# Summing clipped rows: the last four rows in four loads, each shared by ScalarE and VectorE

## The chip, the cores and the metric

The kernel runs on one core of one Trainium2 chip. Its time is device time in microseconds (us), the median of several runs. A core has engines with instruction queues of their own: here ScalarE (ACT in the profile), VectorE (DVE) and SyncE (SP), which issues every DMA. TensorE and GpSimd do none of the work. Engines and DMAs are kept in order by semaphores alone: a load adds 16 to its semaphore when all its data has landed, an instruction of an engine adds 1 when its result is written.

## The reference

```python
def setup_inputs():
    batch, seq, dim = 32, 512, 1024
    return {"x": np.random.randn(batch, seq, dim).astype(np.float32)}

def reference(x):
    relu_x = np.maximum(x, 0)
    return np.sum(relu_x, axis=-1).astype(np.float32)
```

So 16,384 rows of 1,024 float32 numbers are clipped at zero and summed, row by row. 67.1 MB are read, 64 KB are written.

## The kernel before

Each of the 128 partitions holds 128 rows (NT), and its sums are gathered in `res`, a column for each row. Three buffers (`bufs`, called `io` in the profile) hold 16 rows of each partition. Seven full loads of 16 rows go round these buffers, and a load into a buffer waits for the sums of what was in it. The last 16 rows come in pieces: loads of 8 and of 4 rows (`TAIL`), and then the last four rows, which the change is about.

There are three ways to sum a row, each a small helper in `relu_sum`:

- `clamp` and `total` (lines 115 to 131): ScalarE clips many rows in place, and VectorE then adds them up, one instruction each. This is done for the first 92 rows of a partition.
- `act_row` (lines 133 to 139): ScalarE clips one row and adds it up in one instruction, ACTIVATE, with a short second one, ACTIVATION_READ_ACCUMULATOR, which writes the sum and raises the semaphore `act`.
- `dve_row` (lines 141 to 155): VectorE does the same with TENSOR_SCALAR_CACHE_REDUCE and DVE_READ_ACCUMULATOR, and raises `dve`.

The order within each queue is the order in which the program is written; there is no planner. All loads are issued by SP in order (line 99), each with a semaphore of its own, and share the 16 DMA engines of one queue, so they land in the order of issue. Behind the loads SP has three stores (`store`, lines 106 to 113). Each store is a wait for `act` as an instruction of its own (line 109) and then the DMA, which itself waits for `dve` (line 110). The first store has the sums of rows 0 to 15, the second those up to the first two of the last four rows, the third those of the last two.

The last four rows, called r0 to r3 here, are 4 x 1,024 columns in a partition. Before the change they come in four loads (lines 204 to 217), in this order:

1. 2,328 columns: r0, r1 and the first 280 of r2 (`START_PIECE`). ScalarE sums r0; VectorE sums r1 and then the 280.
2. 1,284 columns: the last 260 of r2 (`END_PIECE`) and all of r3. ScalarE sums r3, VectorE the 260.
3. 240 columns of r2, into a buffer of their own (`piece`). VectorE sums them.
4. 244 columns of r2, into another buffer. VectorE sums them (lines 226 to 235) together with three columns behind them, in which the three partial sums of r2 stand.

Clipping leaves a partial sum as it is, since it is not negative, so the last instruction gives the sum of r2. It waits for the last load in an instruction of its own and for VectorE's own partial sums in itself. ScalarE has no part in it.

Of the kernel before, what the change touches and what calls it, by code (L numbers as in the profile page):

```python
# [4 lines left out]
F32 = mybir.dt.float32  # L5
RELU = mybir.ActivationFunctionType.Relu
MAX, ADD = mybir.AluOpType.max, mybir.AluOpType.add
P = 128

ROWS = 16  # L10
# [3 lines left out]
TWO = [[16], [16], [16], [8, 8], [8, 8], [7, 7], []]  # L14
# [3 lines left out]


TAIL = [8, 4]  # L20
START_PIECE, END_PIECE = 280, 260
PIECES = [240, 244]

EARLY = 1

# [1 line left out]
def kernel(tc: tile.TileContext, x: bass.AP, out: bass.AP):  # L27
    nc = tc.nc
    sems = Semaphores(tc)

    tc.close()
    tc.compile()
    nc.cur_bb = nc.bb_map[tc.start_bb_name]
    body = nc.cur_bb.bb.instructions
    ends = list(body)
    body.clear()
    n_stores = relu_sum(nc, sems, x, out)
    body.extend(ends)


    nc.cur_bb = nc.bb_map[tc.start_bb_name + "_end"]
    nc.cur_bb.bb.instructions.clear()
    nums = sorted(s.num for s in (*sems.loads, sems.act, sems.dve))
    cleared = range(nums[0], nums[-1] + 1)
    assert len(cleared) == len(nums)
    nc.sync.sem_clear(cleared)
    nc.sync.wait_ge(sems.stored, 16 * n_stores).then_inc(sems.stored, -16 * n_stores)
    open_without_barrier(tc, EARLY)


class Semaphores:
    def __init__(self, tc: tile.TileContext):
        n = len(TWO) + len(TAIL) + 2 + len(PIECES)
        self.loads = [tc.alloc_semaphore(f"load{i}") for i in range(n)]
        self.act = tc.alloc_semaphore("act")
        self.dve = tc.alloc_semaphore("dve")
        self.stored = tc.alloc_semaphore("stored")


def relu_sum(nc, sems: Semaphores, x: bass.AP, out: bass.AP):  # L60
    x_flat = x.flatten_outer_dims()
    N, D = x_flat.shape
    NT = N // P
    NB = len(TWO)
    assert N == P * NT == P * ROWS * (NB + 1)
    assert sum(TAIL) == ROWS - 4 and START_PIECE + END_PIECE + sum(PIECES) == D

    bufs = [nc.alloc_sbuf_tensor(f"io{i}", [P, ROWS, D], F32) for i in range(NBUF)]
    res = nc.alloc_sbuf_tensor("res", [P, NT], F32)

    extra = len(PIECES) + 1
    parts = [
        nc.alloc_sbuf_tensor(f"piece{i}", [P, w + extra * (i + 1 == len(PIECES))], F32)
        for i, w in enumerate(PIECES)
    ]


    N1 = P * ROWS
# [6 lines left out]
    def rows(m, n):  # L85
        if m < ROWS:
            return xf[:, m : m + n, :]
        return xv[:, m - ROWS : m - ROWS + n, :]
# [8 lines left out]
    def load(dst, src, after=None):  # L97
        nonlocal n_load
        dma = nc.sync.dma_start(out=dst, in_=src)  # L99
        if after:  # L100
            dma.wait_op(sems.dve, after[1], "sem-ge")
        dma.then_inc(sems.loads[n_load], 16)
        n_load += 1
        return sems.loads[n_load - 1]

    def store(m, n, act, dve):
        nonlocal n_store
        dst, src = sums(m, n)
        nc.sync.wait_ge(sems.act, act)
        nc.sync.dma_start(out=dst, in_=src).wait_op(sems.dve, dve, "sem-ge").then_inc(  # L110
            sems.stored, 16
        )
        n_store += 1
# [19 lines left out]
    def act_row(ap, accum_out, loaded):  # L133
        nonlocal n_act
        i = nc.scalar.activation(out=ap, in_=ap, func=RELU, accum_out=accum_out)  # L135
        if loaded is not None:
            i.wait_op(loaded, 16, "sem-ge")
        i.then_inc(sems.act, 1)
        n_act += 1

    def dve_row(ap, accum_out, loaded):
        nonlocal n_dve
        i = nc.vector.tensor_scalar(  # L143
            out=ap,
            in0=ap,
            scalar1=0.0,
            scalar2=None,
            op0=MAX,
            op1=ADD,
            accum_out=accum_out,  # L150
        )
        if loaded is not None:
            i.wait_op(loaded, 16, "sem-ge")
        i.then_inc(sems.dve, 1)
        n_dve += 1

    freed = []
    m = 0
    for j in range(NB):
        buf = bufs[j % NBUF]  # L160
        loaded = load(buf[:, :, :], rows(m, ROWS), j >= NBUF and freed[j - NBUF])
        c = 0
# [19 lines left out]
    buf = bufs[NB % NBUF]  # L182
    c = 0
    for n in TAIL:
        loaded = load(
            buf[:, c : c + n, :], rows(m, n), None if c else freed[NB - NBUF]
        )
# [8 lines left out]
    flat = buf[:, :, :].rearrange("p c d -> p (c d)")  # L196
    src = rows(m, 4).rearrange("p c d -> p (c d)")
    at = c * D
    split = 2 * D
    b = split + START_PIECE  # L200
    end = split + D - END_PIECE
    last, w = parts[-1], PIECES[-1]
    others = [last[:, w + i : w + i + 1] for i in range(extra)]
    loaded = load(flat[:, at : at + b], src[:, :b])
    act_row(buf[:, c, :], res[:, m : m + 1], loaded)
    sums_act = n_act
    dve_row(buf[:, c + 1, :], res[:, m + 1 : m + 2], loaded)
    sums_dve = n_dve
    dve_row(flat[:, at + split : at + b], others[0], None)
    loaded = load(flat[:, at + end : at + 4 * D], src[:, end:])  # L210
    act_row(buf[:, c + 3, :], res[:, m + 3 : m + 4], loaded)
    dve_row(flat[:, at + end : at + 3 * D], others[1], loaded)
    arrived = []
    for part, n in zip(parts, PIECES):
        arrived.append(load(part[:, :n], src[:, b : b + n]))
        b += n
    assert b == end

    store(0, ROWS, *freed[0])
    store(ROWS, NT - ROWS - 2, sums_act, sums_dve)

    for i in range(len(PIECES) - 1):
        dve_row(parts[i][:, :], others[2 + i], arrived[i])
    nc.vector.wait_ge(arrived[-1], 16)
    nc.vector.tensor_scalar(  # L227
        out=last[:, :],
        in0=last[:, :],
        scalar1=0.0,  # L230
        scalar2=None,
        op0=MAX,
        op1=ADD,
        accum_out=res[:, NT - 2 : NT - 1],
    ).wait_op(sems.dve, n_dve, "sem-ge").then_inc(sems.dve, 1)
    n_dve += 1
    store(NT - 2, 2, n_act, n_dve)
    return n_store

# [48 lines left out]
```

## Time and profile before

| | |
|---|---|
| Runs | 161.22, 161.13 and 160.91 us, median 161.13 |
| Span of the profiled execution | 159.84 us |
| Its own time | not listed apart; median less span leaves 1.29 us around the span |
| DMA queue | 67.18 MB, busy 97.9% of the span |
| VectorE, ScalarE | busy 117.6 us (74%) and 104.2 us (65%) |
| Loads 1 to 4 of the last four rows, landed | 155.50, 157.15, 157.45, 157.77 us |
| Last store issued, last store landed | 158.41, 159.80 us |

The span runs from the first instruction, which is the issue of the first load, to the last. A time in the table counts from its start. A load's landing is its issue time and the time to landing that the profile lists for it; the time that an engine starts after a wait on it agrees within 0.03 us.

How to read the rows: a line of the timeline has the start, the length, the engine (ACT, DVE; SPq is SP's queue), the line of the kernel, the operation, what it writes and reads, and, in brackets, how long the engine had been idle and for what. An operation of 128x280 works on 280 columns of 128 partitions. A READ_ACCUMULATOR overlaps the end of the instruction before it, and the next instruction of the engine can begin while it runs.

### The profile page before, as it was taken

What the parts mean: (1) busy time and instruction counts of PE and PEld (TensorE: products, weight loads), DVE (VectorE), ACT (ScalarE), POOL (GpSimd) and SP (SyncE); (2) the same over time, 40 slices, a digit from 0 to 9 for tenths busy, and PEclk for the clock granted to TensorE, in tenths of its full rate; (3) what the DMA queues carried; (4) which work ended last, traced back from release to release, by engine and by line L of the source; (5) the groups of instructions that cost most, each with busy time, mean ns of one, the idle gap of its engine ahead of it and who ended that gap; (6) DMA issues with size and microseconds to landing.
All of it is one profiled execution on the core that took longest, in us unless ns stands there. A gap on an engine that the chain in (4) does not pass through costs nothing.

```text
span 159.8 us, 120 instructions
## 1 busy us (share of the span) xinstructions
DVE 117.6 (74%) x43; ACT 104.2 (65%) x50; POOL 0.2 (0%) x4
## 2 busy tenths in 40 slices
DVE  0000000006999799994999999999999999999986
ACT  0000049993699808996099951999329993499994
POOL 0000000000000000000000000000000000000000
DMA  8996996996996997999989969969969969898993
GB/s 279 508 508 279 525 508 279 525 492 295 525 492 295 525 459 328 525 394 394 525 361 426 525 295 492 525 262 525 508 279 525 508 279 525 377 410 385 425 416 102
DMA packets 2304, 67.18 MB, mean 420 GB/s; under 512 B 640, under 2 KB 896, under 8 KB 1024
## 3 DMA queue, kind: packets, MB, share of 16 engines
q1 hardware_dynamic: 2304, 67.18, 97.9%
HBM read 67.11 MB, written 0.07 MB: 420 GB/s over the span
## 4 chain that ended last, share of the span: by engine, by line
DMA 44%; DVE 33%; ACT 17%; another core or an unknown queue 3%; SPq 1%; issue 0%
DMA io<-in_x_dram 44%; DVE res L128 32%; ACT io L120 17%; SPq L99 1%; DVE io L143 0%; DVE piece L227 0%; DVE piece L143 0%
## 5 line engine op out<-in xcount | busy, mean ns | idle before, releaser
L128 DVE TENSOR_REDUCE res<-io 128x8 f32<-128x8192 f32 (+2 forms) x9 | 101.1, 11286 | 40.2 <-ACT io L120 40.2
L120 ACT ACTIVATE io<-io 128x8192 f32<-128x8192 f32 (+2 forms) x9 | 81.7, 9111 | 26.0 <-DMA io<-in_x_dram 25.9
L135 ACT ACTIVATE io<-io 128x1024 f32<-128x1024 f32 x20 | 20.9, 1044 | 6.1 <-DMA io<-in_x_dram 6.1
L143 DVE TENSOR_SCALAR_CACHE_REDUCE io<-io 128x1024 f32<-128x1024 f32 (+2 forms) x15 | 15.8, 1110 | 0.6 <-DMA io<-in_x_dram 0.4
L118 ACT ACT_TABLE_LOAD x1 | 1.3, 1283 | 22.0 <-DMA io<-in_x_dram 22.0
L135 ACT ACTIVATION_READ_ACCUMULATOR io<-io 128x1 f32 x20 | 3.7, 187 | 0.0
L143 DVE DVE_READ_ACCUMULATOR io<-io 128x1 f32 x15 | 1.2, 82 | 0.0
L227 DVE TENSOR_SCALAR_CACHE_REDUCE piece<-piece 128x247 f32<-128x247 f32 x1 | 0.4, 410 | 0.0
L143 DVE TENSOR_SCALAR_CACHE_REDUCE piece<-piece 128x240 f32<-128x240 f32 x1 | 0.4, 398 | 0.0
L272 POOL MEMSET const-bfloat16-1.0<- 128x1 bf16 x1 | 0.1, 102 | 0.0
L272 POOL MEMSET const-uint8-127<- 128x1 uint8 x1 | 0.1, 102 | 0.0
L272 POOL MEMSET const-float32-1.0<- 128x1 f32 x1 | 0.1, 99 | 0.0
L272 POOL MEMSET const-float32-0.0<- 128x1 f32 x1 | 0.1, 98 | 0.2 <-issue 0.2
L143 DVE DVE_READ_ACCUMULATOR piece<-piece 128x1 f32 x1 | 0.1, 84 | 0.0
L227 DVE DVE_READ_ACCUMULATOR piece<-piece 128x1 f32 x1 | 0.1, 83 | 0.0
## 6 DMA issues: line engine op xcount, KB each, us to landing
io<-in_x_dram SPq DMA_DIRECT2D x1, 4096.0 KB, 21.6
io<-in_x_dram SPq DMA_DIRECT2D x1, 2048.0 KB, 26.1
io<-in_x_dram SPq DMA_DIRECT2D x1, 1164.0 KB, 28.4
io<-in_x_dram SPq DMA_DIRECT2D x1, 642.0 KB, 29.6
piece<-in_x_dram SPq DMA_DIRECT2D x1, 122.0 KB, 29.2
piece<-in_x_dram SPq DMA_DIRECT2D x1, 120.0 KB, 29.4
io<-in_x_dram SPq DMA_DIRECT2D x7, 26.9
out_dram<-res SPq DMA_DIRECT2D x1, 55.0 KB, 1.6
```

The source lines that it names most:

```text
L99: dma = nc.sync.dma_start(out=dst, in_=src)
L118: nc.scalar.preload_act_table(RELU).wait_op(loaded, 16, "sem-ge")
L120: i = nc.scalar.activation(out=ap, in_=ap, func=RELU)
L128: nc.vector.tensor_reduce(out=res[:, m : m + n], in_=ap, axis=mybir.AxisListType.X, op=ADD).wait_op(sems.act, n_act, "sem-ge").then_inc(se ...
L135: i = nc.scalar.activation(out=ap, in_=ap, func=RELU, accum_out=accum_out)
L143: i = nc.vector.tensor_scalar(out=ap, in0=ap, scalar1=0.0, scalar2=None, op0=MAX, op1=ADD, accum_out=accum_out,)
L227: nc.vector.tensor_scalar(out=last[:, :], in0=last[:, :], scalar1=0.0, scalar2=None, op0=MAX, op1=ADD, accum_out=res[:, NT - 2 : NT - 1],) ...
L272: nc = _bacc.Bacc("TRN2", target_bir_lowering=False, num_devices=1)
```

## The change

The four rows still come in four loads, of other sizes and in part in another order, and both engines work on each:

1. 2,304 columns: r0 for ScalarE; r1 and the first 256 of r2 (`HEAD`) for VectorE.
2. 906 columns, the end of r3: the first 276 (`END_DVE`) for VectorE, 630 for ScalarE.
3. 531 columns of r2: 295 (`MIDDLE_DVE`) for VectorE, 236 (`MIDDLE_ACT`) for ScalarE.
4. 355 columns across the border of the two rows, into one buffer `last`: the last 237 of r2 (`LAST_DVE`) for VectorE, the first 118 of r3 (`LAST_ACT`) for ScalarE.

The buffer `last` has three columns ahead of the 355, for r2's partial sums, and two behind them, for r3's. VectorE's last instruction adds up 240 columns (3 + 237), ScalarE's 120 (118 + 2). One of r2's partial sums is now ScalarE's, and one of r3's is VectorE's. So ahead of its last instruction each of the two queues gets two waits as instructions of their own: for all of ScalarE's earlier sums, and for VectorE's (in ScalarE's queue only up to the 276 columns). The wait for the last load stands in the last instruction itself. SP's order is the same: loads, first store, second store, last store.

```diff
-START_PIECE, END_PIECE = 280, 260
-PIECES = [240, 244]
+HEAD = 256
+MIDDLE_DVE, MIDDLE_ACT = 295, 236
+LAST_DVE, LAST_ACT = 237, 118
+END_DVE = 276
...
+    n_last = LAST_DVE + LAST_ACT
+    last = nc.alloc_sbuf_tensor("last", [P, 3 + n_last + 2], F32)
...
-    loaded = load(flat[:, at : at + b], src[:, :b])
+    head = 2 * D + HEAD
+    middle = head + MIDDLE_DVE + MIDDLE_ACT
+    end = middle + n_last
+    dve_sums = [last[:, i : i + 1] for i in range(3)]
+    act_sums = [last[:, 3 + n_last + i : 4 + n_last + i] for i in range(2)]
+    loaded = load(flat[:, at : at + head], src[:, :head])
     act_row(buf[:, c, :], res[:, m : m + 1], loaded)
     sums_act = n_act
     dve_row(buf[:, c + 1, :], res[:, m + 1 : m + 2], loaded)
     sums_dve = n_dve
-    dve_row(flat[:, at + split : at + b], others[0], None)
+    dve_row(flat[:, at + 2 * D : at + head], dve_sums[0], None)
     loaded = load(flat[:, at + end : at + 4 * D], src[:, end:])
-    act_row(buf[:, c + 3, :], res[:, m + 3 : m + 4], loaded)
-    dve_row(flat[:, at + end : at + 3 * D], others[1], loaded)
-    arrived = []
-    for part, n in zip(parts, PIECES):
-        arrived.append(load(part[:, :n], src[:, b : b + n]))
-        b += n
+    split = at + end + END_DVE
+    dve_row(flat[:, at + end : split], act_sums[0], loaded)
+    ends_dve = n_dve
+    act_row(flat[:, split : at + 4 * D], act_sums[1], loaded)
+    loaded = load(flat[:, at + head : at + middle], src[:, head:middle])
+    split = at + head + MIDDLE_DVE
+    dve_row(flat[:, at + head : split], dve_sums[1], loaded)
+    act_row(flat[:, split : at + middle], dve_sums[2], loaded)
+    loaded = load(last[:, 3 : 3 + n_last], src[:, middle:end])
...
-    for i in range(len(PIECES) - 1):
-        dve_row(parts[i][:, :], others[2 + i], arrived[i])
-    nc.vector.wait_ge(arrived[-1], 16)
-    nc.vector.tensor_scalar(
-        out=last[:, :],
...
-    ).wait_op(sems.dve, n_dve, "sem-ge").then_inc(sems.dve, 1)
-    n_dve += 1
+    nc.vector.wait_ge(sems.act, n_act)
+    nc.vector.wait_ge(sems.dve, n_dve)
+    nc.scalar.wait_ge(sems.act, n_act)
+    nc.scalar.wait_ge(sems.dve, ends_dve)
+    dve_row(last[:, : 3 + LAST_DVE], res[:, NT - 2 : NT - 1], loaded)
+    act_row(last[:, 3 + LAST_DVE :], res[:, NT - 1 : NT], loaded)
     store(NT - 2, 2, n_act, n_dve)
```

More of the change, by code (lines that the diff above doesn't have):

```diff
@@ L52, in __init__ @@
     def __init__(self, tc: tile.TileContext):
-        n = len(TWO) + len(TAIL) + 2 + len(PIECES)
+        n = len(TWO) + len(TAIL) + 4
         self.loads = [tc.alloc_semaphore(f"load{i}") for i in range(n)]
@@ L65, in relu_sum @@
     assert N == P * NT == P * ROWS * (NB + 1)
-    assert sum(TAIL) == ROWS - 4 and START_PIECE + END_PIECE + sum(PIECES) == D
+    assert sum(TAIL) == ROWS - 4
+    assert HEAD + MIDDLE_DVE + MIDDLE_ACT + LAST_DVE == D
     bufs = [nc.alloc_sbuf_tensor(f"io{i}", [P, ROWS, D], F32) for i in range(NBUF)]
     res = nc.alloc_sbuf_tensor("res", [P, NT], F32)
[L71 to L75, printed above, removed]
+    n_last = LAST_DVE + LAST_ACT
+    last = nc.alloc_sbuf_tensor("last", [P, 3 + n_last + 2], F32)
     N1 = P * ROWS
@@ L198, in relu_sum @@
     at = c * D
[L199 to L203, printed above, removed]
-    loaded = load(flat[:, at : at + b], src[:, :b])
+    head = 2 * D + HEAD
[4 more added lines that the diff above has]
+    loaded = load(flat[:, at : at + head], src[:, :head])
     act_row(buf[:, c, :], res[:, m : m + 1], loaded)
@@ L208, in relu_sum @@
     sums_dve = n_dve
-    dve_row(flat[:, at + split : at + b], others[0], None)
+    dve_row(flat[:, at + 2 * D : at + head], dve_sums[0], None)
     loaded = load(flat[:, at + end : at + 4 * D], src[:, end:])
-    act_row(buf[:, c + 3, :], res[:, m + 3 : m + 4], loaded)
-    dve_row(flat[:, at + end : at + 3 * D], others[1], loaded)
-    arrived = []
-    for part, n in zip(parts, PIECES):
-        arrived.append(load(part[:, :n], src[:, b : b + n]))
-        b += n
-    assert b == end
+    split = at + end + END_DVE
[7 more added lines that the diff above has]
+    loaded = load(last[:, 3 : 3 + n_last], src[:, middle:end])
     store(0, ROWS, *freed[0])
     store(ROWS, NT - ROWS - 2, sums_act, sums_dve)
-    for i in range(len(PIECES) - 1):
-        dve_row(parts[i][:, :], others[2 + i], arrived[i])
-    nc.vector.wait_ge(arrived[-1], 16)
-    nc.vector.tensor_scalar(
-        out=last[:, :],
[L229 to L234, printed above, removed]
-    ).wait_op(sems.dve, n_dve, "sem-ge").then_inc(sems.dve, 1)
-    n_dve += 1
+    nc.vector.wait_ge(sems.act, n_act)
[4 more added lines that the diff above has]
+    act_row(last[:, 3 + LAST_DVE :], res[:, NT - 1 : NT], loaded)
     store(NT - 2, 2, n_act, n_dve)
```

## The prediction, made before the changed kernel had run

> **What bounds the kernel now.** I read the page first (span, the DMA row, the queue's share), then the chain that ended last, then the timeline of the last 5 us, the groups with their shapes kept apart for the price of an instruction by its columns, and the answers for `piece` and for the single queue waits. The page:
>
> ```profile
> span 159.8 us, 120 instructions
> DMA  8996996996996997999989969969969969898993
> q1 hardware_dynamic: 2304, 67.18, 97.9%
> ```
>
> The DMA queue is busy to the last slice, so the stream of loads sets the time up to where the last load lands, and the change moves no byte out of it. What it can alter is the stretch behind the stream. The end of the chain (start, length, what):
>
> ```profile
> 127.56 29.58 DMA io<-in_x_dram
> 157.15 0.03 issue
> 157.17 0.43 DVE io L143 x2
> 157.60 0.22 DVE piece L143
> 157.82 0.02 issue
> 157.84 0.10 DVE piece L143
> 157.94 0.02 issue
> 157.96 0.42 DVE piece L227 x2
> ```
>
> From the landing of load 2 at 157.15 on, the chain is VectorE's: 260 columns, 240, and the closing 247, which starts at 157.96 although load 4 had landed at 157.77 (issue 128.54 and 29.2 us to landing). So 0.19 us is VectorE being behind the data. The timeline shows both engines:
>
> ```profile
> 155.53 1.06 ACT L135 ACTIVATE io<-io 128x1024 f32<-128x1024 f32 x1 [0.31 <-DMA io<-in_x_dram]
> 155.53 1.22 DVE L143 TENSOR_SCALAR_CACHE_REDUCE io<-io 128x1024 f32<-128x1024 f32 x1 [0.44 <-DMA io<-in_x_dram]
> ...
> 156.67 0.44 DVE L143 TENSOR_SCALAR_CACHE_REDUCE io<-io 128x280 f32<-128x280 f32 x1
> ...
> 157.17 1.06 ACT L135 ACTIVATE io<-io 128x1024 f32<-128x1024 f32 x1 [0.49 <-DMA io<-in_x_dram]
> 157.17 0.42 DVE L143 TENSOR_SCALAR_CACHE_REDUCE io<-io 128x260 f32<-128x260 f32 x1
> ...
> 157.52 0.40 DVE L143 TENSOR_SCALAR_CACHE_REDUCE piece<-piece 128x240 f32<-128x240 f32 x1
> ...
> 157.96 0.41 DVE L227 TENSOR_SCALAR_CACHE_REDUCE piece<-piece 128x247 f32<-128x247 f32 x1
> 158.13 0.19 ACT L135 ACTIVATION_READ_ACCUMULATOR io<-io 128x1 f32 x1
> 158.30 0.08 DVE L227 DVE_READ_ACCUMULATOR piece<-piece 128x1 f32 x1
> ```
>
> ScalarE ends r3 at 158.32, VectorE r2 at 158.38: two paths within 0.06 us. The last store is issued at 158.41 and lands at 159.80; the span ends at 159.84. These 1.43 us stay as they are: same store, same size.
>
> **Prices, from this profile.** VectorE: 1,024 columns take 1,220 ns, 280 take 440, 240 take 398, so 1.04 ns a column and 150 fixed. The next one can start 78 ns + 1.04 a column after a start (157.17 to 157.52 for 260). Its sum is out about 170 ns + 1.04 a column after the start (157.96 to 158.39 for 247). For ScalarE the trace has long rows only:
>
> ```profile
> L120 ACT ACTIVATE io<-io 128x16384 f32<-128x16384 f32 x3 | 41.6, 13857 | 9.7 <-DMA io<-in_x_dram 9.7
> L120 ACT ACTIVATE io<-io 128x8192 f32<-128x8192 f32 x4 | 27.9, 7022 | 10.9 <-DMA io<-in_x_dram 10.9
> ```
>
> (13,857 - 7,022) / 8,192 = 0.834 ns a column; 1,057 ns for 1,024 after a wait leaves 203 fixed, and 1,042 back to back leaves 188. The sum is out 304 ns + 0.834 a column after the start (157.17 to 158.32 is 1.15, and 0.01 to the semaphore). Loads: 240 columns in 157.15 to 157.45 and 244 in 157.45 to 157.77, 1.28 and 1.31 ns a column; 1,284 in 1.65, 1.28. I take 1.285, with no fixed part to be seen between 240 and 1,284 columns.
>
> **The change part by part.** *Loads.* Four for four, issued by SP 30 us ahead, the same 4,096 columns: load 4 still lands at 157.77. Backwards from there: load 3 at 157.77 - 355 x 1.285 = 157.31, load 2 at 157.31 - 0.68 = 156.63, load 1 at 156.63 - 1.16 = 155.47. SP's three stores keep their places, and the second waits for the same two sums (r0, r1), so it goes out near 156.78 again, beside the last loads as before. Cost: nothing, covered by the stream. What isn't covered: `last` puts the 355 columns 12 bytes into a row of 1,440, a place no load here has. From below 0; from above, packets at half rate, 0.46 us (355 x 1.285 once more). I take 0: the loads of 240, 244 and 1,284 columns, from three different places in memory, have one rate.
>
> At this point a page speaks against the uneven cuts. The Trainium skill, DMA: Bandwidth & Descriptors, How a descriptor splits into AXI transactions, says that a read which starts off a 256-byte boundary fetches from the boundary below. By it the three loads before would waste 240, 96 and 32 bytes a row, those after 216, 0 and 76, 76 bytes fewer in all, 0.02 us as an estimate at the rate above; the rows show no trace of either.
>
> *VectorE.* Five instructions for five. r1 starts at 155.50, the 256 at 156.64, the 276 at 156.99 (load 2 is in), the 295 at 157.35 (load 3 landed at 157.31). Its sum is out at 157.35 + 0.31 + 0.17 = 157.83. In the old order 260 + 240 was out at 157.94.
>
> *ScalarE.* Two instructions become four. r0 from 155.50, free at 156.55. The 630 wait for load 2 and start at 156.65; 525 + 202 ns later, at 157.38, the 236 can start (load 3 is in); sum out at 157.38 + 0.20 + 0.29 = 157.87. That is 0.10 behind load 4 and 0.04 behind VectorE.
>
> The Trainium skill, ScalarE: Activation LUTs, Rules for kernel authors, budgets some 0.3 us for each ACTIVATE besides its columns. By that the 630, the 236 and the closing 120 would each cost 0.1 more than here, 0.3 us in all; the 1,057 ns of the 1,024 columns leave 0.2.
>
> *The two waits in each queue.* Both closing instructions now stand behind ScalarE's 236. Nothing else is queued behind these waits, but SP's last store waits for both. VectorE's single queue wait of before (line 226) lasts 21 ns, SP's 17; how long a queue needs from one such wait to its next instruction the trace shows on SP alone: the first store's wait at 129.04, its DMA at 129.11, so 65 ns a step. Bounds: 0.025 us in all, if the waits are as cheap as the start after a landing (157.15 to 157.17), and 0.03 + 2 x 0.065 = 0.16. I take the upper end, as it is the nearer row, an instruction wait with something directly behind it. The closing pair starts at 157.87 + 0.16 = 158.03 (157.90 at the lower end); load 4 is long in.
>
> *The close.* VectorE's 240: sum out 0.42 later (157.52 to 157.94 before), 158.45. ScalarE's 120: 0.10 + 0.30, 158.43. SP's wait for `act` sees that at 158.45 and needs 0.065 to the DMA: 158.51 or so, VectorE being done by then. Before: 158.41. So the last store goes out 0.10 us later; at the lower end (158.38) 0.03 earlier. Since each step rounds by some 0.01, I set +0.09.
>
> *Sum.* Span 159.84 + 0.09 = 159.93. The profiled execution's own time isn't listed; the median less its span, 1.29, is taken as what lies around it: 161.22 against 161.13. The new split frees VectorE of 0.11 us, and the joint with ScalarE and the waits take it back.
>
> **The rivals.** *A, the forecast:* +0.09, 161.22. *B, the waits are hidden and ScalarE is not late:* with the closing pair at 157.80, right behind load 4, the store goes out at 158.28, 0.13 earlier: 161.00. For it: ScalarE is late by 0.10 only in my sum, and 0.03 in load 2's landing counts in full. Against: the fixed 0.2 of each ACTIVATE. It is the most that the tail has to give. *C, ScalarE becomes the bound (slower):* three ACTIVATEs in a row stand between load 2 and the end, and no short one is in the trace. At 0.1 us more for each, 0.3 in all, 161.52; with A's 0.09 it decides from 0.08 each. Against: the fixed part is 203 at 1,024 columns and 195 to 204 at 8,192 and 16,384, so nothing says that it grows below. *D, load 4 lands late* through its odd place: doubled to 158.23, the waits then being over, closing pair at 158.25, ScalarE's sum at 158.65, store at 158.73: +0.32, 161.45. It decides only at a full doubling, or together with a later load 3. *E, the change does nothing that counts,* the two ends staying at 158.4: 161.13, counted under A.
>
> **How the numbers follow.** The three runs of before lie from 160.91 to 161.22; 0.2%, 0.32 us, is about what a measurement of this kernel can tell from no change. A and E: 0.62, of which 0.58 within, 0.02 on either side by the runs' own scatter. B: 0.16, of which 0.05 faster, should the stream run early as in the run of 160.91. C: 0.13, of which 0.11 slower. D: 0.09, slower. Together 0.07 faster, 0.71 within, 0.22 slower. Range: from below B's 161.00 by a little scatter, 160.95, to just over C's 161.52, 161.55. The likeliest case alone: 161.00 to 161.42.
>
> **What would show it.** Right: load 4 lands within 0.05 of 157.77 by the same rate; the 630 start at some 156.65 and the 236 directly behind them; both closing instructions start within 0.05 of each other and 0.1 to 0.25 after load 4; the last store is issued between 158.38 and 158.55. B: they start within 0.04 of load 4. C: ACTIVATEs of 236 and 120 columns that take much over 400 and 300 ns. D: over 0.5 us between the landings of loads 3 and 4. I am wrong altogether if anything ahead of 155.4 moves, since the loads and sums up to there are the same.

## The result, and the profile after

| | before | after |
|---|---|---|
| Time, median of 10 runs each, side by side | 161.06 us (160.91 to 161.22) | 161.44 us (161.26 to 161.66) |
| Ratio to before | | 1.0023, 95% interval 1.0013 to 1.0032 |
| Span of the profiled execution | 159.84 us | 159.81 us |
| Loads 1 to 4 of the last four rows, landed | 155.50, 157.15, 157.45, 157.77 us | 155.44, 156.58, 157.27, 157.72 us |
| Last store issued | 158.41 us | 158.37 us |

The changed kernel is slower by 0.38 us. The odd thing is that its profile does not show it: the span is no longer than before. The page of the changed kernel starts like this:

```profile
span 159.8 us, 125 instructions
...
DVE 117.6 (74%) x43; ACT 104.7 (65%) x54; POOL 0.2 (0%) x4
...
q1 hardware_dynamic: 2304, 67.18, 97.9%
```

ScalarE has four instructions more that count as work (54 against 50), and with its queue wait five more in all (55 against 50 in the trace); VectorE has 44 in both. The DMA queue moved the same bytes in the same time. The timeline of the changed kernel's end (start, length, engine, line, operation; idle time before it in brackets):

```profile
155.47 1.06 ACT L139 ACTIVATE io<-io 128x1024 f32<-128x1024 f32 x1 [0.29 <-DMA io<-in_x_dram]
...
156.60 0.73 ACT L139 ACTIVATE io<-io 128x630 f32<-128x630 f32 x1
...
156.95 0.44 DVE L147 TENSOR_SCALAR_CACHE_REDUCE io<-io 128x276 f32<-128x276 f32 x1
...
157.31 0.45 DVE L147 TENSOR_SCALAR_CACHE_REDUCE io<-io 128x295 f32<-128x295 f32 x1
157.33 0.38 ACT L139 ACTIVATE io<-io 128x236 f32<-128x236 f32 x1
...
157.89 0.30 ACT L139 ACTIVATE last<-last 128x120 f32<-128x120 f32 x1
157.93 0.40 DVE L147 TENSOR_SCALAR_CACHE_REDUCE last<-last 128x240 f32<-128x240 f32 x1 [0.16 <-ACT io L139]
158.10 0.19 ACT L139 ACTIVATION_READ_ACCUMULATOR last<-last 128x1 f32 x1
158.26 0.08 DVE L147 DVE_READ_ACCUMULATOR last<-last 128x1 f32 x1
```

Both engines keep pace with the data up to the last piece. Then both wait: load 4 is in at 157.72, VectorE's 295 columns are out at 157.79 and ScalarE's 236 at 157.82, but the closing pair starts at 157.89 and 157.93. The chain that ended last of the changed kernel shows this joint as its only pieces (start, length, what): the wait in VectorE's queue, the way from there to the engine, and the closing sum.

```profile
157.82 0.05 DVEq L233
157.86 0.07 issue
157.93 0.41 DVE last L147 x2
```

How far the tail follows the stream can be told apart from the stream's own scatter: take the issue of the last store less the landing of load 4. Before it is 158.41 - 157.77 = 0.64, after 158.37 - 157.72 = 0.65. The tail alone gives no 0.38 us. So the first question is whether the loss lies inside the span at all.

### The profile page after: what moved, and what is told of

Same layout as the page of the kernel before. It is cut to its first block, busy times and chain, and to the rows that moved or that the text cites. A ratio compares the mean times of both kernels' runs of the same rounds, so it can differ in the third digit from the quotient of the medians.

```text
span 159.8 us, 125 instructions
## 1 busy us (share of the span) xinstructions
DVE 117.6 (74%) x43; ACT 104.7 (65%) x54; POOL 0.2 (0%) x4
## 2 busy tenths in 40 slices
DMA packets 2304, 67.18 MB, mean 420 GB/s; under 512 B 640, under 2 KB 768, under 8 KB 1024
## 3 DMA queue, kind: packets, MB, share of 16 engines
q1 hardware_dynamic: 2304, 67.18, 97.9%
## 5 line engine op out<-in xcount | busy, mean ns | idle before, releaser
L139 ACT ACTIVATE io<-io 128x1024 f32<-128x1024 f32 (+2 forms) x21 | 20.9, 998 | 5.6 <-DMA io<-in_x_dram 5.6
L147 DVE TENSOR_SCALAR_CACHE_REDUCE io<-io 128x1024 f32<-128x1024 f32 (+3 forms) x16 | 16.1, 1068 | 0.5 <-DMA io<-in_x_dram 0.4
```

What stands on the lines that cost most here:

```text
L147: i = nc.vector.tensor_scalar(out=ap, in0=ap, scalar1=0.0, scalar2=None, op0=MAX, op1=ADD, accum_out=accum_out,)
```

## The experiments

Each ratio below is to the kernel before, on the same chip and in the same series. "Around the span" is the time of an execution less its span, as a mean over all executions of a kernel; each of them lists both, the span to 0.1 us. "Program" is the number of instructions in an engine's compiled program; before it is 54 for ScalarE and 48 for VectorE, after 59 and 48. The traces record four fewer for each: 50 and 44, 55 and 44.

**Both kernels once more, for the spans of all their executions.** No edit.

> The kernel before, unchanged, run again for the spans of its executions, which the first profile does not set against a time. Theory 1 (the span carries the loss): its time stays near 161.1 and its spans are some 0.3 us shorter than the 159.8 of the changed kernel, 159.4 to 159.5, so that the first profile of before was of a slow execution. Theory 2 (the loss lies around the span): its spans are 159.8 and its time less its span is 1.3, against 1.65 for the changed kernel.

> The changed kernel, unchanged, on the same chip as the run of before. Both theories: 161.4, ratio 1.002 to before, time less span 1.65. If the ratio is within 1.001 of one, the loss of the first comparison belonged to that chip.

| | time, median | ratio, 95% interval | span, mean | around the span |
|---|---|---|---|---|
| before again | 161.08 us | 0.9999, 0.9990 to 1.0008 | 159.72 us | 1.34 us |
| after again | 161.33 us | 1.0016, 1.0007 to 1.0026 | 159.75 us | 1.64 us |

Theory 2 held. The spans of the two kernels differ by 0.03 us, less than the executions of one of them scatter (159.6 to 160.0 us). The time around the span is 1.34 in one kernel and 1.64 in the other, and in the ten executions of the first comparison it was 1.65. The loss is there again on this chip, a little smaller.

**The place of the last load.** It goes 64 bytes into its rows instead of 12:

```diff
-    last = nc.alloc_sbuf_tensor("last", [P, 3 + n_last + 2], F32)
+    last = nc.alloc_sbuf_tensor("last", [P, 16 + n_last + 2], F32)
...
-    loaded = load(last[:, 3 : 3 + n_last], src[:, middle:end])
+    loaded = load(last[:, 16 : 16 + n_last], src[:, middle:end])
```

> The changed kernel with the last load put 64 bytes into its rows in place of 12 bytes, all else as it was. If the odd place of the last load costs the 0.38 us: 161.1. If not, as I expect from its landing at 157.72 in the profile of the changed kernel: 161.4.

Measured: 161.42 us, ratio 1.0019 (1.0011 to 1.0028), around the span 1.65. The place costs nothing that this shows: loads 3 and 4 land 0.45 us apart in both.

**The cuts.** In the kernel before:

```diff
-START_PIECE, END_PIECE = 280, 260
-PIECES = [240, 244]
+START_PIECE, END_PIECE = 283, 258
+PIECES = [241, 242]
```

> The kernel before with its cuts moved by one to three columns, so that the last three loads are read from places that are no multiple of 16 bytes; the work of the engines and the number of loads stay. If the uneven cuts cost the 0.38 us: 161.4 to 161.5. If not, as I expect: 161.1.

Measured: 161.13 us, ratio 1.0006 (0.9997 to 1.0014), around the span 1.35, and the last load lands 0.33 us after the one before it, against 0.32. Uneven cuts do not bring the 0.3 us; a cost of 0.1% of the time is not excluded by the interval.

**A longer program for ScalarE, and nothing else.** Ten waits on the load of the sixth buffer go into ScalarE's queue, behind the 14 rows of this buffer that `clamp` and `total` sum (the last of 94 such rows, not 92). The work ahead of them has already waited for this load. The ten become five instructions: one single wait and four pairs; the tenth wait stands in the row behind them itself.

```diff
+        for i in range(10 if j == 5 else 0):
+            nc.scalar.wait_ge(loaded, 16)
         for _ in range(ACT[j]):
```

> The kernel before, its four loads and its split of the work unchanged, with ten waits on an already landed load put into ScalarE's queue some 25 us ahead of the end, where ScalarE then sits idle for 5 us; they make five more instructions, 59 in place of 54, as many as the changed kernel has. Theory 1 (ScalarE's longer program costs time around the span): time less span goes from 1.34 to about 1.65, the span stays at 159.6 to 159.8, time 161.4. Theory 2 (the loss belongs to what ScalarE does at the end, its short instructions or its waits): time less span stays 1.34, time 161.1.

Measured: 161.37 us, ratio 1.0017 (1.0008 to 1.0026), span 159.70, around it 1.67. This is the decisive run. The loads, the split, the tail and the span are those of the kernel before, and yet the loss is there in full. The added waits by their line (shortest, middle and longest duration in ns, then the first and last start):

```profile
L170 ACTq EVENT_SEMAPHORE  x5: 17/38/38, 118.7 to 119.0; - x5
```

The rows around their place in the program, from the timeline of this kernel:

```profile
124.75 6.16 ACT L120 ACTIVATE io<-io 128x7168 f32<-128x7168 f32 x1
...
130.82 1.04 ACT L135 ACTIVATE io<-io 128x1024 f32<-128x1024 f32 x1
...
131.86 1.04 ACT L135 ACTIVATE io<-io 128x1024 f32<-128x1024 f32 x1
132.80 0.19 ACT L135 ACTIVATION_READ_ACCUMULATOR io<-io 128x1 f32 x1
...
138.02 1.06 ACT L135 ACTIVATE io<-io 128x1024 f32<-128x1024 f32 x1 [5.03 <-DMA io<-in_x_dram]
```

ScalarE's queue ran ahead of the engine: it passed the waits at 118.7 to 119.0 us, 41 us ahead of the end and not 25, while the engine still had 12 us of work in front of the row behind them. This row starts at 130.82, just before the 7,168 columns end, as it did without the waits, and ScalarE idles for the same 5.03 us after the two rows. So the waits took no time inside the span.

**How long is too long.** The same with five waits (56 instructions) and with twenty (64):

> The same with five waits, which make two more instructions, 56. Theory 1 as a price for each instruction, 0.06 us: time less span about 1.46, time 161.2. Theory 1 as a step at some length: 1.34 or 1.65. Theory 2: 1.34.

> The kernel before with twenty waits on a landed load in ScalarE's idle stretch, 64 instructions in its program. So far time less span was 1.35 at 54 to 57, 1.51 at 58 and 1.65 at 59. If every instruction past 57 costs 0.15 us: 1.35 + 7 x 0.15 = 2.4, time 162.1. If it was a step that is over at 59: 1.66, time 161.4. The span itself stays at 159.7 in both.

Measured: with 56, 161.05 us, ratio 0.9999 (0.9990 to 1.0008), around the span 1.34. With 64, 161.21 us, ratio 1.0012 (1.0003 to 1.0022), around the span 1.50 as a mean, but from 1.34 to 1.66 from one execution to the next, where all others stay within some 0.1 of their mean. So it is neither a price for each instruction (2.4 was expected) nor a step that stays at 1.66.

**A longer program for VectorE.** Fills of a spare buffer at the start of its queue, five and ten of them:

```diff
+    spare = nc.alloc_sbuf_tensor("spare", [P, 8], F32)
+    for i in range(5):
+        nc.vector.memset(spare[:, i : i + 1], 0.0)
```

> The kernel before with five more instructions in VectorE's queue, small fills of a spare buffer at its very start, where VectorE waits for 35 us; 53 in place of 48. If the length of any engine's program costs time around the span: time less span 1.65, time 161.4. If only ScalarE's does, or only the longest program's (ScalarE's 54): 1.34 and 161.1.

> The kernel before with ten fills of a spare buffer at the start of VectorE's queue, 58 instructions in VectorE's program, ScalarE's 54. With 53 time less span was 1.43. If VectorE's program has its own bend, at 52 or 53, and the same price: 1.43 + 5 x 0.15 = 2.2, time 161.9. If only the two programs' sum counts (102 before, 107 with 53, 107 in the changed kernel, which had 1.65): 1.35 + 0.3 or more, but then the 53 should have had 1.65 too. If the 0.08 was all: 1.43, time 161.1.

Measured: with 53 instructions 161.07 us, ratio 0.9995 (0.9986 to 1.0005), around the span 1.43; with 58, 161.38 us, ratio 1.0022 (1.0012 to 1.0031), around the span 1.64. The effect is not ScalarE's own. Neither expectation had its size right: with 58 it is not the 2.2 of a constant price, and it stops at the same 1.64 to 1.67 as with ScalarE. The sum of both programs does not set it either: 107 gave 1.43 here and 1.64 to 1.67 with ScalarE's longer one.

**ScalarE without its share of the third load.** VectorE sums all 531 columns; nothing of ScalarE's is waited for ahead of VectorE's last instruction.

```diff
-MIDDLE_DVE, MIDDLE_ACT = 295, 236
+MIDDLE_DVE, MIDDLE_ACT = 531, 0
...
-    act_row(flat[:, split : at + middle], dve_sums[2], loaded)
...
-    nc.vector.wait_ge(sems.act, n_act)
+    nc.vector.wait_ge(sems.dve, ends_dve)
```

> The changed kernel with all 531 columns of the third load summed by VectorE, so that ScalarE has two instructions fewer, 57, and nothing of ScalarE's is waited for ahead of VectorE's last instruction. In the span: VectorE's partial sum comes at 157.31 + 0.55 + 0.17 = 158.03 in place of 157.79, its last instruction starts at some 158.1 in place of 157.93, so the span is 0.15 longer. Around the span: by a price for each instruction 1.34 + 3 x 0.06 = 1.53; by a step, 1.34 or 1.65; by theory 2, between 1.34 and 1.65 as far as the waits or the short sums count.

Measured: 161.29 us, ratio 1.0017 (1.0008 to 1.0026). It is as slow as the changed kernel, but for the other reason: around the span 1.35 (57 instructions), span 159.97. From its timeline:

```profile
157.18 0.70 DVE L147 TENSOR_SCALAR_CACHE_REDUCE io<-io 128x531 f32<-128x531 f32 x1
157.61 0.30 ACT L139 ACTIVATE last<-last 128x120 f32<-128x120 f32 x1 [0.33 <-DMA last<-in_x_dram]
...
158.04 0.40 DVE L147 TENSOR_SCALAR_CACHE_REDUCE last<-last 128x239 f32<-128x239 f32 x1 [0.16 <-DVE io L147]
```

ScalarE closes as soon as load 4 is in (157.58), VectorE 0.43 later. The last store goes out 0.90 us after load 4, 0.25 more than in the changed kernel. So ScalarE's share of the third load does its work: without it the span is 0.2 longer than that of the changed kernel (159.75 to 159.79), where I had expected 0.15, and this uses up what the shorter program gives.

**The waits in the queue.** The same loads and split as the changed kernel, but the five partial sums raise the semaphore of the last load, and the closing pair waits for the sum of both in one:

```diff
-    dve_row(flat[:, at + head : split], dve_sums[1], loaded)
-    act_row(flat[:, split : at + middle], dve_sums[2], loaded)
+    dve_row(flat[:, at + head : split], dve_sums[1], loaded, 16, last_load)
+    act_row(flat[:, split : at + middle], dve_sums[2], loaded, 16, last_load)
...
-    nc.vector.wait_ge(sems.act, n_act)
-    nc.vector.wait_ge(sems.dve, n_dve)
-    nc.scalar.wait_ge(sems.act, n_act)
-    nc.scalar.wait_ge(sems.dve, ends_dve)
-    dve_row(last[:, : 3 + LAST_DVE], res[:, NT - 2 : NT - 1], loaded)
-    act_row(last[:, 3 + LAST_DVE :], res[:, NT - 1 : NT], loaded)
+    dve_row(last[:, : 3 + LAST_DVE], res[:, NT - 2 : NT - 1], loaded, 21)
+    act_row(last[:, 3 + LAST_DVE :], res[:, NT - 1 : NT], loaded, 21)
```

> The changed kernel with the same loads and the same split, but without the two waits as instructions of their own: the five partial sums raise the last load's semaphore, and each closing instruction waits in itself for 16 + 5 on it. ScalarE's program is 58 instructions. In the span: the closing pair starts 0.03 after ScalarE's 236 columns are out, 157.84 in place of 157.89 and 157.93, so the last store goes out 0.09 earlier than in the changed kernel; if the waits in the queue cost nothing, no change. Around the span: if the step of ScalarE's program lies above 58, time less span is 1.35 and the time 161.0; if it lies between 57 and 58, 1.65 and 161.3.

Measured: 161.18 us, ratio 1.0008 (0.9999 to 1.0017). Its timeline has both closing instructions at one time:

```profile
157.49 0.38 ACT L139 ACTIVATE io<-io 128x236 f32<-128x236 f32 x1
...
158.00 0.30 ACT L139 ACTIVATE last<-last 128x120 f32<-128x120 f32 x1
158.00 0.40 DVE L150 TENSOR_SCALAR_CACHE_REDUCE last<-last 128x240 f32<-128x240 f32 x1
```

The last partial sum is out at 157.975, so the start follows 0.02 later, where the changed kernel needs 0.12 on VectorE (157.816 to 157.933) and 0.08 on ScalarE. The store goes out 0.59 after load 4, against 0.65: a gain of 0.06 of the 0.09 expected. Around the span it has 1.51, with 58 instructions: between the two values that I had named.

**A version without the joint and with a short program.** Each engine sums columns of its own row alone; four loads of 2,368, 844, 404 and 480 columns, the last one across the border:

```diff
-HEAD = 256
-MIDDLE_DVE, MIDDLE_ACT = 295, 236
-LAST_DVE, LAST_ACT = 237, 118
-END_DVE = 276
+HEAD, MIDDLE = 320, 404
+LAST_DVE, LAST_ACT = 300, 180
...
+    act_row(flat[:, at + end : at + 4 * D], last[:, 2 + n_last :], loaded, 16, last_load)
...
+    dve_row(flat[:, at + head : at + middle], last[:, 1:2], loaded, 16, last_load)
...
+    dve_row(last[:, : 2 + LAST_DVE], res[:, NT - 2 : NT - 1], loaded, 19)
+    act_row(last[:, 2 + LAST_DVE :], res[:, NT - 1 : NT], loaded, 19)
```

> A candidate to beat both kernels: loads of 2,368, 844, 404 and 480 columns, the last one across the border of the two rows and shared as in the changed kernel, but each engine sums columns of its own row alone, so that no partial sum crosses; both closing instructions wait for 16 + 3 on the last load's semaphore. ScalarE's program is 56 instructions, below the step. VectorE: r1 to 156.69, 320 to 157.10, 404 from 157.15, its sum out at 157.74; closing pair at 157.77, sums out at 158.22 (ScalarE) and 158.25, last store at 158.30 against 158.41 before. Time less span 1.35, so 160.95 to 161.0, against 161.07. If the tail has nothing more to give: 161.07. If a short program is not what counts: 161.3.

From its timeline:

```profile
156.60 0.91 ACT L137 ACTIVATE io<-io 128x844 f32<-128x844 f32 x1
...
157.13 0.57 DVE L148 TENSOR_SCALAR_CACHE_REDUCE io<-io 128x404 f32<-128x404 f32 x1
...
157.76 0.35 ACT L137 ACTIVATE last<-last 128x181 f32<-128x181 f32 x1 [0.16 <-DVE io L148]
157.76 0.47 DVE L148 TENSOR_SCALAR_CACHE_REDUCE last<-last 128x302 f32<-128x302 f32 x1
```

Both close 0.02 after load 4 (157.74), and the store goes out 0.54 after it, at 158.28; 158.30 was expected. With the tail of before it is 0.58 to 0.64 in seven profiles (two of the kernel itself, five with added instructions). Measured: 160.98 us against 161.04, ratio 0.9997 (0.9988 to 1.0006), around the span 1.35. Clearly faster than the changed kernel; against the one before it gains 0.07 us in the tail and 0.06 in the medians, which is within what the comparison can tell.

All programs together:

| program of ScalarE / VectorE | kernel | around the span |
|---|---|---|
| 54 / 48 | before | 1.34 to 1.35 us |
| 54 / 48 | uneven cuts | 1.35 |
| 56 / 48 | five waits | 1.34 |
| 56 / 45 | own rows | 1.35 |
| 57 / 48 | third load to VectorE | 1.35 |
| 58 / 47 | joint in one semaphore | 1.51 |
| 59 / 48 | changed kernel (twice), and with its last load moved | 1.64 to 1.65 |
| 59 / 48 | ten waits | 1.67 |
| 64 / 48 | twenty waits | 1.50 (1.34 to 1.66) |
| 54 / 53 | five fills | 1.43 |
| 54 / 58 | ten fills | 1.64 |

## Why the prediction was right, and where it was wrong

The time fell into the range (160.95 to 161.55) and 0.22 above the forecast of 161.22. The direction was right. Whether the change stays within 0.2%, as the forecast held likeliest, is not decided: it is 0.23% in the first comparison, 0.16% in the second, and both intervals hold 0.2%. But most of the loss is in a place where the sum had none. The time is above the likeliest case's own 161.00 to 161.42; the range reached further for rival C alone, whose cause is not there, so that the time lies in it is luck. Rivals C and D even named 161.52 and 161.45, and the signs of both are absent: the short ACTIVATEs took 383 and 302 ns, and loads 3 and 4 landed 0.45 us apart. Step by step:

- *Loads, "cost: nothing".* Right. Load 4 landed at 157.72 for 157.77, loads 2 and 3 at 156.58 and 157.27 for 156.63 and 157.31, all 0.04 to 0.05 early with the stream. The odd place and the uneven cuts cost nothing that can be seen, as the moved load and the uneven cuts of the kernel before showed. The rule of the Trainium skill on the 256-byte boundary (DMA: Bandwidth & Descriptors, How a descriptor splits into AXI transactions) would have moved the sum by 0.02, to earlier, as an estimate. The packets in the traces show no such cost: if `x` itself starts on such a boundary, packets that start on one took 87 ns for 2,124 bytes and 351 for 9,312 (medians), and packets of 5,136 bytes that start 240 past one took 198, which lies on the line between them, where 240 bytes more would be 9 ns.
- *VectorE.* Right: 295 columns from 157.31 (157.35 forecast), out at 157.79 (157.83), early by as much as the loads.
- *ScalarE.* Right, although the trace of before had no short instruction: 630, 236 and 120 columns took 728, 383 and 302 ns, so 203, 186 and 202 besides 0.834 a column. (The 195 to 204 that the forecast names for the long rows does not come out of its own price: 7,022 and 13,857 ns leave 190 and 193.) The 0.3 us for each ACTIVATE of the Trainium skill (ScalarE: Activation LUTs, Rules for kernel authors) stands there for one whose bias is a `[128,1]` pointer operand, a condition that the forecast left out; `act_row` passes no bias, and the rows of this trace were the better guide. Rival C's price, 0.1 us more for each, is in no run.
- *The two waits, 0.16.* The mechanism was right, the size too large. Two waits that follow one another are one instruction here, 0.05 long on VectorE. VectorE's start came 0.12 behind ScalarE's sum, ScalarE's own 0.08. Where the wait stands in the instruction itself, it is 0.02.
- *The close, +0.09 in the span.* Too large: the store went out 0.65 to 0.66 after load 4 in three profiles of the change, 0.61 as a mean over those seven with the old tail, so +0.04; the mean spans differ by 0.03. Measured from load 4, the new split saves VectorE 0.10 on its partial sums (out 0.07 after it, where it was 0.17), and the joint takes it back, as the sum said: VectorE's last instruction starts 0.21 after load 4, before it was 0.19. The last store went out at 158.37, just ahead of the 158.38 to 158.55 that the forecast named, since the stream was 0.05 early.
- *"The median less its span, 1.29, is taken as what lies around it".* Here it failed. I carried this term over unchanged, and it was the one that counted most: from 1.34 to 1.65 us, 0.31 of the 0.38. It was also 0.05 off from the start, since it set the median of several runs against the span of one slower execution. None of the rivals had it, since all looked inside the span.

That added instructions alone cause such a loss is shown: ten waits without any work, 41 us ahead of the end, do the same to the kernel before, and so do ten fills at the start of VectorE's queue. That they are the cause in the changed kernel too follows from its variants: with 57 instructions, the queue waits at the end kept, the loss around the span is gone, and with 58 and no such waits half of it is there.

What takes the time is not shown. It lies outside what the profile's instructions cover, and the record does not say at which events the device time begins and ends. The semaphore events that the traces have beside the span do not show it: the nine in the last 0.4 us ahead of it lie at the same places to some 3 ns in all fourteen traces, and the last one behind it comes 1.435 to 1.439 us after its end in thirteen of them, with short programs and long. The fourteenth is that of the 64 instructions: its last event comes at 1.481, and it alone has a packet of 8,192 bytes of instructions behind the span, at 160.91 us, as every trace has several ahead of it. So a fetch may play a part there, but ScalarE's 59 and VectorE's 58 lose the time without one behind the span. It depends on the length in no simple way: nothing up to 57 for ScalarE, full at 59, and at 64 sometimes there and sometimes not. Whether the length itself counts, or where the program's end falls in memory or in a fetch, stays open.

## What to carry to other kernels

For a change of some tenths of a microsecond, set every execution's time against its own span before the timeline is read: a loss around the span is found in no view of it, and a kernel with the old work and as many idle instructions tells whether the program's length is the cause. Count instructions as well as microseconds when a tail is cut finer. Where several partial results and a load must be in before one instruction, let them raise one semaphore and wait for the total in the instruction itself: the start follows by 0.02 us rather than 0.08 to 0.12, and the program is shorter. The lengths from 53 to 59 at which time was lost belong to this kernel; no run shows them in another.

## What the runs showed of the hardware that I had not expected

- The time around the span is not a constant of the machine: 1.34 us with ScalarE's program at 54 to 57 instructions, 1.51 at 58, 1.64 to 1.67 at 59; 1.43 and 1.64 with VectorE's at 53 and 58.
- Two waits in a row in one queue are a single instruction with two conditions; it took 0.05 us on VectorE, and 0.07 more went by until the next instruction started there.
- ScalarE's queue passed waits whose condition held 12 us before the engine came to the instruction behind them (118.7 to 119.0 us against 130.82).
- An engine's instruction can raise a semaphore that a load raises too, and one wait for the total of 19 or 21 was followed by the start after 0.02 us.
